# Weaving the adaLN products of a four-layer diffusion backbone: other rates in layers 1 and 2, and layer 0's scale and shift all on TensorE

## The chip, the cores and the metric

The kernel runs on one core of one Trainium2 chip. The metric is device time in microseconds, from the median of three runs. The profile is one further execution of the same program, taken by the hardware profiler. Engines are named as the profile names them: PE is TensorE (PEld its weight loads), DVE VectorE, ACT ScalarE, POOL GpSimd, SP the SyncE queue that issues nearly all DMAs.

## The reference

Two streams of 256 tokens of width 2048, a context (stream 0) and a latent (stream 1), pass through four layers. Their mixers are, in turn, a Fourier transform over tokens and channel groups, a bidirectional mLSTM, grouped-query attention, and the Fourier mixer again. Every layer begins with a modulated norm whose shift, scale and gate come from one conditioning vector per stream:

```python
sc, sc_ctx = silu(c), silu(c_ctx)
for i in range(4):
    shift, scale, gate = split(sc @ ada_w[i] + ada_b[i], 3)        # ada_w[i]: 2048 x 6144
    hx = rmsnorm(x, norm_g[i]) * (1 + scale) + shift
    shift_c, scale_c, gate_c = split(sc_ctx @ ada_w[i] + ada_b[i], 3)
    hc = rmsnorm(ctx, norm_g[i]) * (1 + scale_c) + shift_c
    y_x, y_c = mixer(hx, hc)              # layer 0: (fourier(h) * silu(h @ w_gate)) @ w_out
    x = x + gate * y_x
    ctx = ctx + gate_c * y_c              # not after the last layer
return rmsnorm(x, final_g)
```

The lines `sc @ ada_w[i]` and `sc_ctx @ ada_w[i]` are the adaLN products. `ada_w` is 50 MB of fp32 per layer, read once, for two vectors: it is all memory traffic and hardly any arithmetic. Everything else is matmul of 256 or 512 tokens with 2048-wide weights.

## The kernel before

Activations lie transposed: channel on partitions, token on the free axis, 16 tiles of 128 channels x 512 tokens. All large products run in three passes of fp32r: an operand is split into a rounded part and a remainder (`h`, `l` for activations, `wh`, `wl` for weights), and PE adds h*wh, h*wl and l*wh. ACT makes the rounded part, DVE the remainder.

`gemm` (L262) computes one 512-wide block of outputs over all 16 channel tiles: 8 weight tiles (`wraw`, 512 KB each, two channel tiles in each) and four PSUM banks, 192 matmuls of 512 columns. `make_w` (L244) loads the next weight tile, has ACT round it (L253) and DVE subtract (L254); four raw buffers and three pairs `wh`, `wl` make the prefetch. The weight blocks follow in a fixed list (L238): in layer 0 four blocks of the gate projection and four of the out projection, in layer 1 four pairs of heads with the four blocks qk, v, o, z each and then four out blocks, in layer 2 k, v, four q, four z, four out, in layer 3 four gate and four out.

PE's order is the order in which the program is written. What other engines do, and the order of the DMAs on the SP queue, a planner puts in order, by program order and its own costs; `issue_after(pace[-1])` (L213) holds an adaLN instruction on DVE behind the newest weight split. Woven work is kept in three queues of Python generators, `fill`, `bg` and `adq` (class `Weave`, L91). `run` (L120) steps through a gemm, which yields 32 times, and at each yield gives each queue a credit; a whole credit takes one step of that queue. The credits are the constants of line 27 and 28. `finish` takes all steps up to a key at once, and so sets a deadline.

The adaLN products have two forms:

- `ada_pe` (L170), a chunk of 256 outputs for both vectors: four loads of 512 KB (`araw`, ring of 4), 32 matmuls of 32 weight columns x 256 (L184), a copy by ACT (L188), two transposes (L192), a reduction on DVE (L194). It yields four times.
- `ada_dve` (L198), rows of `ada_w` transposed: a step is one load of 512 KB (same ring), and for each of `nv` streams one multiply with accumulation on DVE (L214) of 128x1024 against `cb`, the conditioning vectors repeated over all partitions.

Head of layer 0, before: `cb` is made by eight `spread` calls (L225: a diagonal by DVE, four transposes, a copy). Tokens `xt` (4 MB) arrive token-major; ACT squares them (L582), `r0` is the inverse norm, DVE scales them (L636). Then a loop over eight pairs `k2` of channel tiles (L637 to L647): scale chunk, shift chunk, then `turned(k2)` is queued on `fill`, which transposes two channel tiles (L612), modulates and splits them, and takes four pieces of the first gemm. Scale and shift are `ada_pe` chunks, but for the shift of `k2` in `DV0` = 2, 4, 6, which is `ada_dve`. At k2 = 1, 3, 5 a Fourier group (`mixed`) is queued on `mixes`. After the loop the first gemm ends, and three more gate blocks and four out blocks follow. During these, at rate BR0, the 4 gate chunks of layer 0 (`ga0`) and the second half of layer 1's scale and shift chunks (`l1`, from `order[NPE1:]`) run on DVE, and at rate AR0 the first half of layer 1's on PE (`adq`, eight `ada_pe` chunks).

Layer 1 onward: all adaLN products are `ada_dve`, queued on `bg` in the order ga1, l2, ga2, l3, ga3, with 32, 64, 32, 64 and 32 steps; ga1 and l2 do two streams in a step, the others one. They are woven at BR1 = 0.3 in every block of layer 1 (L947 to L971), 0.25 in layer 2 (L1112, L1123, L1134), 0.12 in its out projection. Deadlines: ga1 before the out projection of layer 1, l2 after it, ga2 and l3 likewise around layer 2's. In layer 2 the k and q blocks end in `qk_norm` (L1005), a chain of ACT and DVE operations on the PSUM bank, whose result PE transposes (L1036) for the attention steps woven in next.

Of the kernel before, what the change touches and what calls it, by code (L numbers as in the profile page):

```python
# [48 lines left out]
def _build(tc, nc, top, A, out):  # L49
# [119 lines left out]

    def ada_pe(l, s, c, cpad, place):  # L170
# [3 lines left out]
        for k2 in range(2):  # L174
            raws = []
            for kq in (2 * k2, 2 * k2 + 1):
                pp, tag, bufs = next(place[0])
                raw = pp.tile([P, 2, 512], F32, tag=tag, name="araw", bufs=bufs)
                Q.dma_start(raw, A["ada_p"][l, s * 8 + c, kq])
                raws.append(raw.rearrange("p a b -> p (a b)").rearrange("p (q n) -> p q n", q=4))  # L180
            for i, rv in enumerate(raws):
                kq = 2 * k2 + i
                for q in range(4):
                    T.matmul(ps[32 * q:32 * q + 32, :256], cpad[:, 4 * kq + q, :], rv[:, q, :],  # L184
                             start=kq == 0, stop=kq == 3)
            yield 1
# [375 lines left out]
    with ExitStack() as st:  # L562
# [11 lines left out]
        ss = p0.tile([P, 4, 4], F32, name="ss")
        xt = []
        for j in range(4):
            x = p0.tile([P, 4, 512], F32, tag="xf", name="xt", bufs=5)
            Q.dma_start(x, A["xtok"][j])
            xt.append(x)
            for i in range(4):  # L580
                junk = p0.tile([P, 512], F32, tag="mu2", name="junk", bufs=2)
# [786 lines left out]
```

## Time and profile before

| | us |
|---|---|
| time, median of 3 runs (lowest to highest) | 2164.38 (2164.37 to 2164.82) |
| the profiled execution's own time | 2165.99 |
| its span, first to last instruction | 2164.1 |
| PE busy in the span | 2094.9 |
| DVE busy | 1523.5 |
| ACT busy | 813.8 |
| mean granted TensorE clock | 0.986 |

451.5 MB move in the span, nearly all of it read. A busy PE is not always a PE at full speed: matmuls overlap, and in stretches where the clock is granted at half the same matmul takes twice as long. So PE's busy time is read together with the row of the granted clock, and a stage is judged by its own rows, not by the share over the whole span.

### The profile page before, as it was taken

What the parts mean: (1) busy time and instruction counts of PE and PEld (TensorE: products, weight loads), DVE (VectorE), ACT (ScalarE), POOL (GpSimd) and SP (SyncE); (2) the same over time, 40 slices, a digit from 0 to 9 for tenths busy, and PEclk for the clock granted to TensorE, in tenths of its full rate; (3) what the DMA queues carried; (4) which work ended last, traced back from release to release, by engine and by line L of the source; (5) the groups of instructions that cost most, each with busy time, mean ns of one, the idle gap of its engine ahead of it and who ended that gap; (6) DMA issues with size and microseconds to landing.
All of it is one profiled execution on the core that took longest, in us unless ns stands there. A gap on an engine that the chain in (4) does not pass through costs nothing. (4 is left out here: it accounts for less than half of the span.)

```text
span 2164.1 us, 29349 instructions
## 1 busy us (share of the span) xinstructions
PE 2094.9 (97%) x11190; PEld 1728.6 (80%) x11190; DVE 1523.5 (70%) x2793; ACT 813.8 (38%) x1338; POOL 17.3 (1%) x29
## 2 busy tenths in 40 slices
PE   6899999999999999999999999999999999999998
PEld 3568777788788888888888888888777777999986
DVE  4867898856697778787664667646665766777666
ACT  4332242224333323322332343224345554545444
POOL 0000000000000000000000000000000000000000
PEclk7999999999999999999999999999999999999999
DMA  9775778972465666576555667763464556764464
GB/s 341 279 265 194 251 273 286 320 261 94 156 205 175 204 202 196 186 230 214 195 191 199 199 222 247 273 215 98 146 218 148 183 190 205 240 208 137 156 195 147
DMA packets 126126, 451.51 MB, mean 209 GB/s; under 512 B 14224, under 2 KB 16784, under 8 KB 123296
## 3 DMA queue, kind: packets, MB, share of 16 engines
q1 hardware_dynamic: 125696, 448.71, 61.7%
q8 instruction: 88, 1.44, 0.3%
q10 hardware_dynamic: 288, 0.92, 0.1%
q14 instruction: 54, 0.44, 0.1%
HBM read 435.91 MB, written 13.66 MB: 208 GB/s over the span
## 5 line engine op out<-in xcount | busy, mean ns | idle before, releaser
L254 DVE TENSOR_TENSOR wl<-wraw,wh 128x1024 fp32r<-128x1024 f32 x400 | 488.7, 1222 | 438.4 <-ACT wh L253 427.2
L295 PE MATMUL acc<-h,wh 128*128 128x512 f32 (+1 forms) x1936 | 688.5, 356 | 6.1 <-ACT h L392 3.9
L253 ACT CAST wh<-wraw 128x1024 fp32r<-128x1024 f32 x400 | 419.4, 1049 | 720.5 <-PE acc L295 617.9
L295 PE MATMUL acc<-l,wh 128*128 128x512 f32 (+1 forms) x1936 | 670.9, 347 | 3.7 <-DVE l L358 1.9
L295 PE MATMUL acc<-h,wl 128*128 128x512 f32 (+1 forms) x1936 | 669.7, 346 | 1.0 <-DVE wl L254 0.9
L295 PE MATMUL acc<-wh,h 128*128 128x512 f32 x1024 | 428.7, 419 | 5.3 <-DVE am L217 3.7
L295 PEld LDWEIGHTS acc<-h,wh 128*128 128x128 f32 x1936 | 367.0, 190 | 61.9 <-issue 11.5
L295 PEld LDWEIGHTS acc<-l,wh 128*128 128x128 f32 x1936 | 366.6, 189 | 51.8 <-DVE l L393 3.5
L295 PEld LDWEIGHTS acc<-h,wl 128*128 128x128 f32 x1936 | 367.1, 190 | 45.1 <-issue 1.7
L295 PE MATMUL acc<-wh,l 128*128 128x512 f32 x1024 | 401.8, 392 | 0.5 <-DVE l L393 0.5
L295 PE MATMUL acc<-wl,h 128*128 128x512 f32 x1024 | 400.6, 391 | 0.0
L214 DVE SCALAR_TENSOR_TENSOR araw<-araw,cb 128x1024 f32<-128x1024 f32 x300 | 365.4, 1222 | 1.9
L295 PEld LDWEIGHTS acc<-wh,h 128*128 128x128 f32 x1024 | 193.5, 189 | 54.7 <-issue 17.1
L295 PEld LDWEIGHTS acc<-wl,h 128*128 128x128 f32 x1024 | 193.6, 189 | 45.3 <-issue 8.4
L295 PEld LDWEIGHTS acc<-wh,l 128*128 128x128 f32 x1024 | 193.0, 188 | 43.1 <-DVE l L393 1.4
L214 DVE SCALAR_TENSOR_TENSOR ajunk<-araw,cb 128x1024 f32<-128x1024 f32 x172 | 209.9, 1220 | 0.0
L184 PE MATMUL xb<-araw,cpad 128*32 128x256 f32 x672 | 56.2, 437 | 15.3 <-DMA araw<-in_ada_p_dram 15.2
L184 PEld LDWEIGHTS xb<-araw,cpad 128*32 128x32 f32 x672 | 17.7, 116 | 44.5 <-DMA araw<-in_ada_p_dram 27.4
L392 ACT ACTIVATE h<-mu,ada 128x256 fp32r<-128x256 f32 x80 | 36.9, 502 | 35.9 <-DVE mu L391 35.9
L845 PE MATMUL xb<-v,wt 128*128 128x256 f32 x192 | 46.7, 379 | 0.0
L450 ACT ACTIVATE sq<-rn 128x256 f32<-128x256 f32 (+1 forms) x48 | 24.7, 515 | 55.4 <-DVE rn L444 53.4
L905 ACT ACTIVATE jk<-yp 128x256 f32<-128x256 f32 x32 | 13.3, 416 | 78.0 <-DVE yp L903 78.0
(223 smaller groups left out, 1485.4 us busy)
## 6 DMA issues: line engine op xcount, KB each, us to landing
araw<-in_ada_t_dram SPq DMA_DIRECT2D x300, 512.0 KB, 5.0
wraw<-in_w1in_dram SPq DMA_DIRECT2D x128, 512.0 KB, 4.0
araw<-in_ada_p_dram SPq DMA_DIRECT2D x84, 512.0 KB, 5.4
wraw<-in_w2in_dram SPq DMA_DIRECT2D x80, 512.0 KB, 3.6
wraw<-in_w0g_dram SPq DMA_DIRECT2D x32, 512.0 KB, 5.6
wraw<-in_w0o_dram SPq DMA_DIRECT2D x32, 512.0 KB, 5.5
wraw<-in_w1o_dram SPq DMA_DIRECT2D x32, 512.0 KB, 4.2
wraw<-in_w2o_dram SPq DMA_DIRECT2D x32, 512.0 KB, 4.0
```

Source lines behind the costliest of these rows:

```text
L184: T.matmul(ps[32 * q:32 * q + 32, :256], cpad[:, 4 * kq + q, :], rv[:, q, :], start=kq == 0, stop=kq == 3)
L214: V.scalar_tensor_tensor(o, rv, 1.0, cb[:, v + 2 - nv, part], ALU.mult, ALU.mult, accum_out=am[:, v, i, hf:hf + 1])
L253: S.copy(wh, raw)
L254: pace.append(V.tensor_tensor(wl, raw, wh.bitcast(F32), ALU.subtract).ins)
L295: T.matmul(o, lhsT, rhs, start=start, stop=stop)
L392: S.activation(h[:, c], u, AF.Identity, bias=ada[:, l, SH, s, kt:kt + 1])
L450: S.activation(sq[:, c], rn[:, b, c], AF.Square)
L845: T.matmul(po[:, :256], wt[:, 128 * k:128 * k + 128], c.v[:, k, 256 * hh:256 * hh + 256], start=k == 0, stop=k == nb - 1)
L905: S.activation(jk, ys, AF.Square, accum_out=c.ssq[:, 4 * hh + i:4 * hh + i + 1])
```

## The change

- Layer 0's head: all sixteen scale and shift chunks are `ada_pe` (`DV0` is gone). In k2 < 4 their loads land not in the ring `araw` but in the buffers `l8` to `l15`, which the head does not need yet; each 512 KB come as two loads of 256 KB (`land_l`).
- Layer 0's gate products (`ga0`, and behind them `l1`) are queued ahead of the loop, and DVE takes steps of them at rate BRS = 0.5 in k2 = 1 to 4.
- `cb` is no longer spread by PE: 16 KB of `crow` are loaded repeated to all partitions (2 MB into SBUF), and ACT applies SiLU.
- Tokens: squares and scaling are shared between ACT and DVE; all 64 transposes come at k2 = 0 (`turn`), and the results are parked in the buffers `h0` to `h15`, from which `modulated` reads. The pieces of the first gemm come one k2 earlier; the first weight tile is loaded at k2 = 0.
- Layer 1's products on PE go from eight chunks to four (NPE1 4 to 2); two more groups (16 steps) of them go to DVE. AR0 goes from 0.17 to 0.09.
- Rates: layer 1 by pair and block instead of 0.3 throughout, its out projection 0.5, layer 2 none in v and q and 0.25 in z as before.

```diff
-DV0 = (2, 4, 6)
-NPE1, CORE1, ATT = 4, 0.4, 1.2
-MIX3, MIX0, MIX1, FR0, BR0, BR1, AR0 = 0.55, 0.9, 0.7, 0.8, 0.34, 0.3, 0.17
+NPE1, CORE1, ATT = 2, 0.4, 1.2
+MIX3, MIX0, MIX1, FR0, BR0, AR0, BRS = 0.55, 0.55, 0.7, 0.55, 0.34, 0.09, 0.5
+BR1 = ((0, 0.35, 0.25, 0.25), (0.35, 0.35, 0.25, 0.25), (0.4, 0.4, 0.3, 0.3), (0.5, 0.5, 0.35, 0.35))
+BR1O, BR2 = 0.5, 0.25
...
+    def land(pp, tag, bufs):
+        def get(src):
+            raw = pp.tile([P, 2, 512], F32, tag=tag, name="araw", bufs=bufs)
+            Q.dma_start(raw, src)
+            return [raw[:, 0, :], raw[:, 1, :]]
+        return get
+
+    def land_l(kt):
+        def get(src):
+            raws = [hlp.tile([P, 512], F32, tag=f"l{k}", name=f"lraw{k}") for k in (kt, kt + 1)]
+            for i in range(2):
+                Q.dma_start(raws[i], src[:, i, :])
+            return raws
+        return get
...
-        for v in range(2):
-            for j in range(4):
-                o = cb[:, v, 512 * j:512 * j + 512]
-                drain(spread(lambda ps, o=o: V.tensor_copy(o, ps), cvec[:, v, 4 * j:4 * j + 4]))
...
+            if j == 3:
+                S.activation(dummy, one1, AF.Sqrt)
             for i in range(4):
-                S.activation(junk, x[:, i, :], AF.Square, accum_out=ss[:, i, j:j + 1])
+                if i % 2:
+                    S.activation(junk, x[:, i, :], AF.Square, accum_out=ss[:, i, j:j + 1])
+                else:
+                    V.scalar_tensor_tensor(junk, x[:, i, :], 1.0, x[:, i, :], ALU.mult, ALU.mult,
+                                           accum_out=ss[:, i, j:j + 1])
...
-            def turned(k2):
-                for kt in (2 * k2, 2 * k2 + 1):
...
-                        T.transpose(ps[:, 128 * t:128 * t + 128], xt[j][:, t, 128 * i:128 * i + 128], ident)
...
-                if 0 < k2 <= 6:
-                    for _ in range(4):
-                        next(first)
-                        yield
+            def turn(j):
+                for t in range(4):
+                    if t % 2:
+                        S.activation(xt[j][:, t, :], xt[j][:, t, :], AF.Copy, scale=r0[:, t:t + 1])
+                    else:
+                        V.tensor_scalar(xt[j][:, t, :], xt[j][:, t, :], r0[:, t:t + 1], None, ALU.mult)
+                for i in range(4):
+                    ps = bank()
+                    for t in range(4):
+                        T.transpose(ps[:, 128 * t:128 * t + 128], xt[j][:, t, 128 * i:128 * i + 128], ident)
+                    x = hlp.tile([P, 512], F32, tag=f"h{4 * j + i}", name=f"xT{4 * j + i}")
+                    (S.copy if i % 2 else V.tensor_copy)(x, ps)
+                    xT.append(x)
+            def modulated(k2):
...
+                def pieces():
+                    if k2 < 6:
+                        for _ in range(4):
+                            next(first)
+                            yield
+                return pieces()
...
+            spare = cycle(land_l(kt) for kt in (8, 10, 12, 14))
+            bg.add("ga0", ada_chain([(0, GA, j, 2) for j in range(4)]))
+            bg.add("l1", ada_chain([(1, s, j, 2) for s, j in order[NPE1:]]))
             for k2 in range(8):
                 for s in (SC, SH):
-                    for _ in ada_dve(0, s, 2 * k2, 2, 2) if s == SH and k2 in DV0 else ada_pe(0, s, k2, cpad, [slots]):
-                        fill.give(FR0)
-                        mixes.give(MIX0)
+                    for n, _ in enumerate(ada_pe(0, s, k2, cpad, [spare if k2 < 4 else slots])):
+                        if k2 == 0:
+                            if n == 1:
+                                for j in range(4):
+                                    if (j > 0) == (s == SH):
+                                        turn(j)
+                            if s == SH and n == 1:
+                                make_w()
+                                Q.dma_start(cb, A["crow"].to_broadcast([P, 2 * D]).rearrange("p (v k) -> p v k", v=2))
+                                for v in range(2):
+                                    S.activation(cb[:, v, :], cb[:, v, :], AF.Silu)
+                                Q.dma_start(cst[:, C_CD:], A["cst"][:, C_CD:])
+                        else:
+                            if k2 < 5:
+                                bg.give(BRS)
+                            fill.give(FR0)
+                            mixes.give(MIX0)
                 fill.finish(f"t{k2 - 1}")
-                fill.add(f"t{k2}", turned(k2))
+                fill.add(f"t{k2}", modulated(k2))
...
-            run(gemm(hl, "A", 0, 512, c.done[0]) if p else first, 0.5, BR1 if p else 0)
+            run(gemm(hl, "A", 0, 512, c.done[0]) if p else first, 0.5, BR1[p][0])
...
-            "p (a b) -> p a b", a=4), resid[1], 0, [(0.5, BR1)] * 4, norm=norm)
+            "p (a b) -> p a b", a=4), resid[1], 0, [(0.5, BR1O)] * 4, norm=norm)
...
-        run(gemm(hl, "B", 0, 512, done_vv), 1.0, 0.25)
+        run(gemm(hl, "B", 0, 512, done_vv), 1.0, 0)
...
-            run(gemm(hl, "B", 256, 512, done_q), ATT, 0.25)
+            run(gemm(hl, "B", 256, 512, done_q), ATT, 0)
...
-            run(gemm(hl, "B", 256, 512, done_z2), ATT, 0.25)
+            run(gemm(hl, "B", 256, 512, done_z2), ATT, BR2)
```

More of the change, by code (lines that the diff above doesn't have):

```diff
@@ L2 @@
 from contextlib import ExitStack, nullcontext
-from itertools import repeat
+from itertools import cycle, repeat
 import concourse.bass as bass
@@ L174, in ada_pe @@
         for k2 in range(2):
[L175 to L180, printed above, removed]
+            raws = [next(place[0])(A["ada_p"][l, s * 8 + c, kq]) for kq in (2 * k2, 2 * k2 + 1)]
             for i, rv in enumerate(raws):
@@ L183, in ada_pe @@
                 for q in range(4):
-                    T.matmul(ps[32 * q:32 * q + 32, :256], cpad[:, 4 * kq + q, :], rv[:, q, :],
-                             start=kq == 0, stop=kq == 3)
+                    T.matmul(ps[32 * q:32 * q + 32, :256], cpad[:, 4 * kq + q, :],
+                             rv[q // 2][:, 256 * (q % 2):256 * (q % 2) + 256], start=kq == 0, stop=kq == 3)
             yield 1
@@ L632, in _build @@
             mixes = Weave()
[L633 to L636 removed]
+            slots = repeat(land(ap_, "araw", ARAW))
+            spare = cycle(land_l(kt) for kt in (8, 10, 12, 14))
+            order = [(s, j) for s in (SC, SH) for j in range(4)]
+            bg.add("ga0", ada_chain([(0, GA, j, 2) for j in range(4)]))
+            bg.add("l1", ada_chain([(1, s, j, 2) for s, j in order[NPE1:]]))
             for k2 in range(8):
                 for s in (SC, SH):
[L639 to L641 removed]
+                    for n, _ in enumerate(ada_pe(0, s, k2, cpad, [spare if k2 < 4 else slots])):
[15 more added lines that the diff above has]
+                            mixes.give(MIX0)
                 fill.finish(f"t{k2 - 1}")
[L643 to L645 removed]
+                fill.add(f"t{k2}", modulated(k2))
                 if k2 in (1, 3, 5):
@@ L652, in _build @@
             run(first, MIX1)
-            order = [(s, j) for s in (SC, SH) for j in range(4)]
             place = [slots]
-            bg.add("ga0", ada_chain([(0, GA, j, 2) for j in range(4)]))
-            bg.add("l1", ada_chain([(1, s, j, 2) for s, j in order[NPE1:]]))
             for s, j in order[:NPE1]:
@@ L663, in _build @@
         pa = pool(st, "l0a", reuse_waits="tile")
-        place[0] = repeat((pa, "praw", 2))
+        place[0] = repeat(land(pa, "praw", 2))
         for g in range(2, 4):
@@ L959, in _build @@
             fill.add(f"core{p}", core(c))
-            run(gemm(hl, "B", 0, 512, c.done[2]), CORE1, BR1)
-            run(gemm(hl, "A", 0, 512, c.done[3], used=load_y if p == 3 else None), CORE1, BR1)
+            run(gemm(hl, "B", 0, 512, c.done[2]), CORE1, BR1[p][2])
+            run(gemm(hl, "A", 0, 512, c.done[3], used=load_y if p == 3 else None), CORE1, BR1[p][3])
             fill.finish(f"core{p}")
@@ L1316, in _layout @@
     r["xT"] = np.ascontiguousarray(x.T.reshape(KT, 128, NT).transpose(1, 0, 2))
+    r["crow"] = np.concatenate([g["c_ctx"], g["c"][0]])[None]
     r["cvec"] = np.ascontiguousarray(
```

21 lines of the change are left out of this document (8 added, 13 removed).

## The prediction

> **What bounds the kernel now.** I read the summary first, then the busy time by stage, then who waits for whom in the stages where PE isn't full. The page's first part:
>
> ```profile
> span 2164.1 us, 29349 instructions
> PE 2094.9 (97%) x11190; PEld 1728.6 (80%) x11190; DVE 1523.5 (70%) x2793; ACT 813.8 (38%) x1338; POOL 17.3 (1%) x29
> ```
>
> PE sets the end: 69 us of the span are without it. So there are two ways to gain, less work on PE or less of those 69 us, and each stage must be looked at for itself. The view of busy time by stage (columns: stretch, length, busy time of each engine with its instructions, granted clock, DMA share, GB/s):
>
> ```profile
> 0.00:20.00 20.00, 9.96 (x56) 6.75 (x56) 11.98 (x28) 13.42 (x37) 0.20 (x4) 0.91 0.90 351
> 20.00:45.00 25.00, 17.04 (x132) 5.26 (x128) 11.37 (x32) 4.55 (x10) 0.00 (x0) 0.64 0.93 328
> 45.00:153.50 108.50, 92.21 (x660) 64.75 (x656) 76.03 (x195) 38.82 (x85) 0.00 (x0) 0.91 0.79 280
> 174.00:222.30 48.30, 48.30 (x222) 39.66 (x221) 38.48 (x73) 12.34 (x19) 0.00 (x0) 1.00 0.66 226
> 222.30:459.50 237.20, 237.05 (x1198) 185.93 (x1197) 202.04 (x343) 64.64 (x83) 0.00 (x0) 1.00 0.82 292
> 560.80:915.80 355.00, 355.00 (x1612) 284.93 (x1611) 283.08 (x542) 121.77 (x210) 11.07 (x15) 1.00 0.60 193
> 915.80:1004.70 88.90, 88.90 (x402) 73.63 (x401) 68.00 (x110) 26.93 (x37) 0.00 (x0) 1.00 0.67 217
> 1305.60:1438.00 132.40, 132.40 (x593) 109.66 (x592) 84.84 (x145) 36.11 (x44) 0.00 (x0) 1.00 0.73 251
> 1534.30:1717.40 183.10, 172.04 (x790) 136.55 (x789) 113.18 (x163) 82.64 (x118) 0.00 (x0) 0.96 0.55 181
> ```
>
> The first three rows are layer 0's head up to the last shift chunk: PE lacks 34.3 of 153.5 us, its clock is granted at 0.64 for a time, and DMA is 0.79 to 0.93 busy. The next rows are the rest of layer 0 and layer 1: PE is full, DVE at 85% (202.04 of 237.20) or less. The last is layer 2's v and q blocks: 11.1 us without PE at clock 0.96. The waits in the head, PE's and then the SP queue's (us, times, longest):
>
> ```profile
> PE xb L184 <- DMA araw<-in_ada_p_dram: 15.2, 18, 3.5
> PE xb L233 <- DVE adiag L228: 8.1, 3, 5.1
> ```
>
> ```profile
> SPq L179 <- PE xb L184: 36.5, 28, 4.9
> SPq L179 <- DVE araw L214: 29.9, 9, 7.7
> ```
>
> PE waits for adaLN loads, and the queue that issues them waits for buffers held by PE or by DVE. The head is a matter of bytes and of how many loads are in flight.
>
> **The change part by part.**
>
> *Layer 0's body, PE: gain 9.2 us.* Four `ada_pe` chunks leave a stretch in which PE is full. The groups of instructions there, and one entry of PE's timeline:
>
> ```profile
> L184 PE MATMUL xb<-araw,cpad 128*32 128x256 f32 x224 | 15.0, 385 | 0.0
> L192 PE MATMUL xb<-cst,ar 128*128 128x128 f32 x12 | 2.3, 270 | 0.0
> ```
>
> ```profile
> 230.50 1.07 PE L184 MATMUL xb<-araw,cpad 128*32 128x256 f32 x16
> ```
>
> Sixteen of a chunk's 32 matmuls take 1.07 us (15.0 / 224 x 16 is the same), and a pair of transposes at most 0.38 (2.3 / 6), less where it overlaps its neighbours: 2.3 us a chunk, 9.2 for four. Their share of DVE and ACT (a reduction, a copy) is below a microsecond each. DVE gets 16 steps of `l1` in exchange, but 16 of `ga0`'s 32 steps have gone to the head (32 credits of 0.5), so the body's 64 steps stay 64. DVE's 202 us then stand against 228: 89%, still room. If DVE can't keep that, the gain shrinks; I keep 4 to 9.5.
>
> *Layer 0's head: loss 4 us, the least certain term.* Bytes moved by 153.5 us: 351 x 20 + 328 x 25 + 280 x 108.5 = 45.6 MB. The three `DV0` chunks are the same bytes in either form. New are `crow` (2.1 MB) and sixteen `ga0` loads (8.4 MB), less about 1 MB that ran ahead for them already: 55.1 MB. Against that stand more loads in flight: four in `l8` to `l15` beside four of `araw` in k2 = 1 to 4. The rates that the trace has:
>
> ```profile
> GB/s 415 350 293 390 307 162 163 258 162 329 372 279 314 387 285 168 391 397 396 207 27 254 337 334 20 317 252 400 228 305 372 397 192 62 248 340 273 290 343 205
> araw<-in_ada_p_dram SPq DMA_DIRECT2D x32, 512.0 KB, 4.9
> ```
>
> ```profile
> l<-ytd SPq DMA_DIRECT2D x12, 256.0 KB, 3.7
> araw<-in_ada_t_dram SPq DMA_DIRECT2D x8, 512.0 KB, 5.0
> ```
>
> (45 to 153.5 us in 40 slices, with the head's chunk loads; then two load sizes from the end of layer 1; the last column is us to landing.) At the head's own mean, 297 GB/s, the bytes take 186 us; at 328, the rate when PE did nothing but wait for loads, 168; at 351 157; at 397, of single slices, 139. With eight in flight for two thirds of the bytes I take 345: 160 us, 6 later than now. The first gemm's pieces come one k2 earlier, so fewer are left behind the last chunk: by the order of yields now three pieces of six matmuls, 4 us at 0.23 apart (timeline below). PE already waits for the last splits there, and without pieces before it longer:
>
> ```profile
> PE acc L295 <- DVE l L358: 1.2, 2, 0.8
> ```
>
> I let that give back half of the 4 us. Head: +6 - 2 = +4. The bounds are 139 us (-17) and 186 us (+30).
>
> The other parts of the head cost nothing, since PE has 34 us to spare there: three more chunks (6.9 us), against 32 transposes of `spread` that go; the 64 token transposes only move forward, into the time in which the second and third chunk land. What DVE is given (24 products of 1.2 us in the loop become 32, half the squares and 8 copies) meets a DVE that is busy 76 of 108.5 us. PE's own work up to there, 119.2 us by the three rows and about as much after, stays below the loads' time in every case.
>
> The Trainium skill, page "DMA: Bandwidth & Descriptors", section "Rules for kernel authors", says to coalesce small transfers and to move at least 1 MiB in a DMA; its section "Bandwidth" gives 341 GB/s at 1 MB and 138 at 64 KB. An estimate between these by halvings is 290 for 512 KB and 240 for 256 KB, by which the 16.8 MB that the change loads in halves would take 12 us more, and the sum would be 12 us worse. The rows above speak for less: a half lands in 3.7 us, a whole in 5.0, and both halves are in flight at once.
>
> *Layer 1's rates: 0.* At 32 yields a block, steps to the end of the out projection go from 173 (0.3 x 32 x 18) to 213 (32 x 5.15, the sum of the new rates, and 0.5 x 32 x 3). The tightest place is pair 2's qk and v, where 0.4 for 0.3 gives 6.4 steps more of two products over both blocks. What DVE does there for the products, and in the out projection:
>
> ```profile
> 915.80:1004.70 88.90, 45.48 (x76) 1.00 0.67 217
> 1305.60:1438.00 132.40, 33.74 (x56) 1.00 0.73 251
> ```
>
> (The stage view for L214 alone; half of the instructions are the reading of an accumulator.) A product is 1.20 us. Pair 2: 68.0 + 12.8 x 1.20 = 83.4 of 88.9 us. Out projection: 96 x 0.2 = 19.2 steps of one product, 84.8 + 23 = 108 of 132.4. Neither is full, and PE waits for nothing in these stretches now. If the last few per cent stall the weight split, a few us are lost: 0 to +5.
>
> *Layer 2's v and q without products: gain 8 us.* PE's waits from 1534.3 to 1717.4, then DVE and PE as the v block begins:
>
> ```profile
> PE xb L1063 <- ACT pe L1057: 4.0, 2, 3.3
> PE acc L295 <- DVE am L217: 3.7, 1, 3.7
> PE xb L1036 <- DVE rb L1028: 3.1, 2, 2.0
> ```
>
> ```profile
> 1535.46 1.20 DVE L214 SCALAR_TENSOR_TENSOR araw<-araw,cb 128x1024 f32<-128x1024 f32 x1
> ...
> 1540.20 1.19 DVE L214 SCALAR_TENSOR_TENSOR araw<-araw,cb 128x1024 f32<-128x1024 f32 x1
> ...
> 1541.92 0.68 DVE L1016 TENSOR_TENSOR xn<-acc,r 128x512 f32<-128x512 f32 x1
> ```
>
> ```profile
> 1538.41 0.39 PE L295 MATMUL acc<-wl,h 128*128 128x512 f32 x1
> 1538.64 0.40 PE L295 MATMUL acc<-wh,l 128*128 128x512 f32 x1
> 1542.75 0.76 PE L295 MATMUL acc<-wh,h 128*128 128x512 f32 x1 [3.71 <-DVE am L217]
> 1543.31 0.63 PE L295 MATMUL acc<-wl,h 128*128 128x512 f32 x1
> ```
>
> The 3.7 us wait is for the last bank of k (L1016), queued on DVE behind products. Two of them lie in its way, 2.4 us. The 3.1 us for L1028 are the same chain for the first q block, also with products between; without them I count all 3.1. The 4.0 us for L1057 are exps behind other work of ACT, and stay. After the long wait the next matmul comes 0.56 us later instead of 0.23: the clock is at half. Clock 0.96 over 183.1 us is 7.3 us lost. Of the 11.1 us of waits 5.5 go, so half of it, 3.7; I count 2.5, since a slow spell can begin at a wait that stays. 2.4 + 3.1 + 2.5 = 8. Bounds: 2 (only what stands directly in front) and 18 (all waits and the clock).
>
> A part of this stretch where only the two L1036 waits stand, the longer 2.0 us:
>
> ```profile
> 1607.30:1644.00 36.70, 33.65 (x156) 25.59 (x154) 25.25 (x37) 19.71 (x30) 0.00 (x0) 0.95 0.56 189
> ```
>
> The clock fell there too. The Trainium skill, page "TensorE: Matmul & The Clock Gate", Part 1, puts the halving after an idle window of about 3.4 us; by it the 7.3 us would hang on the waits of 3.7 and 3.3 us alone, about half on the one that goes, and the sum would be 1 us better. The row's 0.95 doesn't agree with a window that long.
>
> *Sum.* -9.2 + 4 + 0 - 8 = -13 us. On the profiled execution's 2165.99 us (span 2164.1 and 1.9 around it) that is 2153; the median of the runs is 1.6 lower, so 2151.
>
> **The rivals.**
>
> 1. *The head's loads decide* (slower). DMA stays at the head's mean rate, because SP is one queue: a `ga0` load that waits for a buffer held by DVE (29.9 us of such waits now) stops every scale and shift load behind it, and in k2 = 4 both share one ring again. The head costs up to +30 instead of +4: 2151 + 26 = 2177. It decides against the change from a rate of 319 GB/s down: then the last chunk comes at 173 us, and the 17.2 us of the other terms are used up. For it: 280 GB/s in the loop now. Against it: 328 with four loads in flight and an idle PE.
> 2. *Layer 2's waits stay*, because weight splits and ACT's rounding stand in the chain too: only 2 of 8 us come, 2157.
> 3. *DVE fills up in layer 0 and layer 1*, the planner putting the products elsewhere than the rates say, so that the four chunks taken from PE come back as waits for weight splits: no gain in the body and up to 5 us lost in layer 1, 2151 + 9 + 5 = 2165, no change. Against it: 89% and 94%.
> 4. *The loads run at 397 GB/s*: the head gains 17, 2130. The slices that reach this are few.
>
> **How the numbers follow.** Forecast 0.50, rival 1 0.18 (half of it at a small loss or none), rival 2 0.17, rival 3 0.08, rival 4 0.07. About 0.2% (4.3 us) is what a measurement of this kernel can tell from no change. Faster: 0.50 + 0.17 + 0.07, and little of the others: 0.76. Same: rival 3 and the near part of rival 1, 0.11. Slower: 0.13. The range reaches to rival 4 and to the middle of rival 1: 2131 to 2171. The likeliest case by itself holds 2141 to 2160.
>
> **What would show it.** Right: the last L184 of the head at about 160 us with 55 MB moved before it; 128 matmuls of L184 after the head instead of 256, and gemms there 2.3 us shorter for each chunk gone; in layer 1 no wait of PE for L254; in v and q no L214 on DVE and no wait for the last k bank above 1.5 us. Wrong: a last chunk after 173 us, SP waiting for L214 longer than 30 us in it, or PE waiting for weight splits anywhere from 560 to 1438 us. The forecast falls with the head's rate first, and then with layer 2.

## The result and the profile after

The changed kernel takes 2169.34 us (median of 8 runs) against 2164.6 us of the kernel before (8 runs as well): ratio 1.0024, 95% interval 1.0014 to 1.0035, so it is slower by 3 to 8 us. The forecast was 2151. The profiled execution took 2168.66 us. In the changed file the lines of the planned work stand some 13 further down: the chunk matmul is L197 (was L184), the chunk's loads L184 (halves, into the `l` buffers) and L175 (the ring), the product on DVE L227 (L214) with its load L220, the weight tile's load, rounding and subtraction L263, L266 and L267 (L250, L253, L254), the gemm matmul L308 (L295), the split of `u` into `h` and `l` L370 and L371 (L357, L358).

The first part of the page after:

```profile
span 2166.9 us, 29317 instructions
PE 2090.5 (96%) x11124; PEld 1726.6 (80%) x11124; DVE 1534.1 (71%) x2803; ACT 822.5 (38%) x1341; POOL 19.0 (1%) x29
```

PE has 4.4 us less work and 7.2 us more without work. The view of busy time by stage after (stretch, length, busy time of PE, PEld, DVE, ACT and POOL, granted clock, DMA share, GB/s); then the same head stretches of the kernel before:

```profile
20.00:60.00 40.00, 32.92 (x233) 17.16 (x233) 26.10 (x54) 22.85 (x36) 0.00 (x0) 0.96 1.04 397
60.00:120.00 60.00, 47.49 (x318) 32.38 (x318) 43.02 (x99) 16.83 (x36) 0.00 (x0) 0.81 0.80 286
120.00:174.20 54.20, 46.03 (x347) 30.47 (x346) 28.98 (x85) 18.05 (x39) 0.00 (x0) 0.89 0.83 301
...
244.60:476.80 232.20, 229.12 (x1096) 183.31 (x1095) 200.29 (x336) 63.63 (x80) 0.00 (x0) 1.00 0.77 267
575.50:930.40 354.90, 354.90 (x1611) 284.94 (x1610) 279.71 (x535) 121.67 (x210) 10.37 (x15) 1.00 0.58 190
930.40:1019.30 88.90, 88.90 (x401) 73.65 (x400) 82.34 (x136) 27.10 (x37) 0.00 (x0) 1.00 0.76 253
1320.30:1452.80 132.50, 132.50 (x594) 109.62 (x593) 105.40 (x186) 35.84 (x44) 0.00 (x0) 1.00 0.88 325
1549.00:1719.40 170.40, 165.80 (x792) 132.85 (x790) 87.58 (x111) 82.49 (x119) 0.00 (x0) 1.00 0.38 124
```

```profile
20.00:60.00 40.00, 28.27 (x197) 12.87 (x194) 19.04 (x48) 9.70 (x21) 0.00 (x0) 0.67 0.90 325
60.00:120.00 60.00, 52.05 (x374) 36.43 (x374) 43.42 (x115) 21.38 (x48) 0.00 (x0) 0.94 0.77 274
120.00:153.60 33.60, 29.02 (x222) 20.80 (x220) 24.93 (x66) 12.29 (x27) 0.00 (x0) 0.95 0.80 275
```

The stages begin where PE starts a gemm, so their shift is the ledger of the change:

| stretch | before, us | after, us | difference | forecast |
|---|---|---|---|---|
| start to the second gemm (layer 0's head and first gemm) | 174.0 | 196.3 | +22.3 | +4 |
| from there to layer 1 (layer 0's body) | 335.7 | 328.1 | -7.6 | -9.2 |
| layer 1 | 975.8 | 975.8 | 0.0 | 0 |
| layer 2's k block | 48.8 | 48.8 | 0.0 | none |
| layer 2's v and q | 183.1 | 170.4 | -12.7 | -8 |
| the rest | 446.7 | 447.5 | +0.8 | none |

The head spoils the sum. Its last scale or shift chunk ends at 174.2 us instead of 153.6. DMA starts at 397 GB/s between 20 and 60 us and then falls to 286, and PE's clock falls with it, to 0.81. PE's and SP's waits in the head after (PE from 0 to 200 us, SP from 0 to 174; us, times, longest):

```profile
PE xb L197 <- ACT junk L595: 16.0, 1, 16.0
PE xb L197 <- DMA araw<-in_ada_p_dram: 9.2, 7, 2.9
PE acc L308 <- ACT h L370: 6.4, 3, 3.0
PE acc L308 <- ACT wh L266: 6.3, 2, 3.3
PE xb L197 <- DMA lraw<-in_ada_p_dram: 3.1, 1, 3.1
PE acc L308 <- DVE wl L267: 2.5, 2, 1.9
PE acc L308 <- DVE l L371: 1.9, 3, 1.5
```

```profile
SPq L175 <- PE xb L197: 31.5, 16, 5.6
SPq L184 <- PE xb L197: 20.2, 16, 7.1
SPq L175 <- DVE araw L227: 13.5, 3, 7.5
```

Before, PE's waits were for loads and for `spread`; now 17.1 us of them stand at L308, at the pieces of the first gemm, which wait for their own operands: `h` and `l` just modulated, `wh` and `wl` just loaded (before, these four came to 4.4 us). SP's waits for L227, by which the slower rival was to be told, fell from 29.9 to 13.5 us.

Layer 0's body and layer 2, after: the chunk matmuls between 196.3 and 524.4 us in the view of groups, PE's only wait from 380 to 477 us, and PE's waits in v and q.

```profile
L197 PE MATMUL xb<-araw,cpad 128*32 128x256 f32 x128 | 8.6, 385 | 0.0
```

```profile
PE acc L308 <- DVE wl L267: 3.1, 2, 1.7
```

```profile
PE acc L308 <- DVE xn L1059: 2.2, 1, 2.2
PE xb L1079 <- DVE rb L1071: 1.4, 2, 1.0
PE xb L1106 <- ACT pe L1100: 1.0, 1, 1.0
```

### The profile page after: what moved, and what is told of

The parts are those of the page before. It is cut to its first block, busy times and chain, and to the rows that moved or that the text cites. A ratio compares the mean times of both kernels' runs of the same rounds, so it can differ in the third digit from the quotient of the medians.

```text
span 2166.9 us, 29317 instructions
## 1 busy us (share of the span) xinstructions
PE 2090.5 (96%) x11124; PEld 1726.6 (80%) x11124; DVE 1534.1 (71%) x2803; ACT 822.5 (38%) x1341; POOL 19.0 (1%) x29
## 5 line engine op out<-in xcount | busy, mean ns | idle before, releaser
L267 DVE TENSOR_TENSOR wl<-wraw,wh 128x1024 fp32r<-128x1024 f32 x400 | 489.7, 1225 | 405.4 <-ACT wh L266 402.4
L308 PE MATMUL acc<-h,wh 128*128 128x512 f32 (+1 forms) x1936 | 691.6, 357 | 16.5 <-ACT h L370 6.4
L266 ACT CAST wh<-wraw 128x1024 fp32r<-128x1024 f32 x400 | 419.3, 1049 | 713.2 <-PE acc L308 560.5
L308 PE MATMUL acc<-l,wh 128*128 128x512 f32 (+1 forms) x1936 | 675.1, 349 | 3.7 <-DVE l L371 1.9
L308 PE MATMUL acc<-h,wl 128*128 128x512 f32 (+1 forms) x1936 | 673.1, 348 | 5.6 <-DVE wl L267 5.6
L308 PE MATMUL acc<-wh,h 128*128 128x512 f32 x1024 | 426.5, 417 | 3.5 <-DVE xn L1059 2.2
L308 PEld LDWEIGHTS acc<-h,wh 128*128 128x128 f32 x1936 | 369.4, 191 | 73.4 <-issue 9.9
L308 PEld LDWEIGHTS acc<-l,wh 128*128 128x128 f32 x1936 | 369.0, 191 | 53.6 <-DVE l L371 4.5
L308 PEld LDWEIGHTS acc<-h,wl 128*128 128x128 f32 x1936 | 369.8, 191 | 51.3 <-DVE wl L267 7.4
L308 PE MATMUL acc<-wh,l 128*128 128x512 f32 x1024 | 400.6, 391 | 0.5 <-DVE l L406 0.5
L308 PE MATMUL acc<-wl,h 128*128 128x512 f32 x1024 | 399.1, 390 | 0.0
L227 DVE SCALAR_TENSOR_TENSOR araw<-araw,cb 128x1024 f32<-128x1024 f32 x304 | 369.7, 1223 | 10.2 <-DMA araw<-in_ada_t_dram 7.7
L308 PEld LDWEIGHTS acc<-wh,h 128*128 128x128 f32 x1024 | 192.5, 188 | 52.1 <-issue 14.6
L308 PEld LDWEIGHTS acc<-wl,h 128*128 128x128 f32 x1024 | 192.7, 188 | 44.4 <-issue 8.4
L308 PEld LDWEIGHTS acc<-wh,l 128*128 128x128 f32 x1024 | 192.2, 188 | 42.7 <-DVE l L406 1.3
L227 DVE SCALAR_TENSOR_TENSOR ajunk<-araw,cb 128x1024 f32<-128x1024 f32 x176 | 215.0, 1222 | 7.0 <-DMA araw<-in_ada_t_dram 7.0
L197 PE MATMUL xb<-lraw,cpad 128*32 128x256 f32 x256 | 29.9, 437 | 19.8 <-ACT junk L595 16.0
L888 PEld LDWEIGHTS xb<-v,wt 128*128 128x128 f32 x192 | 36.3, 189 | 6.1
```

Source lines behind the costliest of these rows:

```text
L227: V.scalar_tensor_tensor(o, rv, 1.0, cb[:, v + 2 - nv, part], ALU.mult, ALU.mult, accum_out=am[:, v, i, hf:hf + 1])
L266: S.copy(wh, raw)
L267: pace.append(V.tensor_tensor(wl, raw, wh.bitcast(F32), ALU.subtract).ins)
L308: T.matmul(o, lhsT, rhs, start=start, stop=stop)
L888: T.matmul(po[:, :256], wt[:, 128 * k:128 * k + 128], c.v[:, k, 256 * hh:256 * hh + 256], start=k == 0, stop=k == nb - 1)
```

## The experiments

Theory A: what the head moves is what it costs, `ga0`'s 16 loads (8.4 MB) above all. Theory B: the head lost its slack. (Later expectations name theories of their own.) A piece of the first gemm that isn't ready stops PE, which works in program order; the chunk behind it can't free its buffers; SP, one queue, stands before the next load; the rate falls. All runs, with the head read from each run's profile (e1 to e4, e5 to e8 and e9 to e12 ran beside the kernel before with 2165.92, 2166.02 and 2166.37 us; the expectations count after's last chunk from 173.8 us, where its last matmul starts, the table has its end):

| run | time, us | ratio to before, 95% interval | last chunk ends | mean GB/s until then | second gemm starts |
|---|---|---|---|---|---|
| before | | | 153.6 | 298 | 174.0 |
| after | 2169.34 | 1.0024 (1.0014 to 1.0035) | 174.2 | 323 | 196.3 |
| e1 rates only | 2154.39 | 0.9943 (0.9928 to 0.9958) | 152.1 | 301 | 172.5 |
| e2 no ga0 in head | 2155.1 | 0.9950 (0.9935 to 0.9965) | 155.4 | 312 | 177.3 |
| e3 pieces late | 2160.21 | 0.9971 (0.9959 to 0.9984) | 165.4 | 334 | 187.7 |
| e4 weights ahead | 2160.89 | 0.9977 (0.9965 to 0.9989) | 168.1 | 335 | 190.3 |
| e5 late and ahead | 2154.81 | 0.9948 (0.9932 to 0.9965) | 159.2 | 348 | 181.6 |
| e6 no ga0, late, ahead | 2147.88 | 0.9925 (0.9904 to 0.9946) | 141.1 | 335 | 163.5 |
| e7 ga0's loads only | 2159.33 | one run | 166.6 | 334 | 188.5 |
| e8 ga0's products only | 2154.1 | one run | 159.6 | 303 | 181.8 |
| e9 eight in flight | 2144.08 | 0.9894 (0.9879 to 0.9909) | 140.0 | 341 | 163.9 |
| e10 all in halves | 2147.3 | 0.9907 (0.9890 to 0.9923) | 145.3 | 325 | 169.2 |
| e11 products to gates | 2151.36 | one run | 159.3 | 345 | 181.6 |
| e12 one group more | 2144.58 | 0.9896 (0.9881 to 0.9911) | 143.6 | 329 | 165.9 |

### Rates only (e1)

The kernel before with the new rates of layers 1 and 2 and nothing of layer 0.

```diff
+BR1 = ((0, 0.35, 0.25, 0.25), (0.35, 0.35, 0.25, 0.25), (0.4, 0.4, 0.3, 0.3), (0.5, 0.5, 0.35, 0.35))
+BR1O, BR2 = 0.5, 0.25
...
-        run(gemm(hl, "B", 0, 512, done_vv), 1.0, 0.25)
+        run(gemm(hl, "B", 0, 512, done_vv), 1.0, 0)
...
```

> The kernel before, with the change's rates for layers 1 and 2 and nothing else of it. By the two traces the stretch from layer 2's v block to its out projection is 13.5 us shorter after the change, layer 1 the same, layer 3's first block 1.5 us longer. If these belong to the rates, this kernel is 12 us faster than before (2152 to 2153 us), with its head unchanged (first gate block ends at 174). If part of it came from what the head does to the order of the products, it gains less, 5 to 8 us.

Measured: 0.57% faster, by the interval 9.1 to 15.6 of 2166 us. Layer 1 keeps its length (976.4 us; 975.8 before); the second q block takes 33.4 us (before 36.7), the third 31.4 (37.5), as they do after, the v block 49.4 (before 51.3, after 47.9). The gain of layer 2 belongs to the rates alone, and the loss to layer 0's head.

The 1.5 us between the two v blocks are the clock's. PE waits 2.2 us for the last k bank in both; here the matmuls behind that wait come 0.42 to 0.46 us apart instead of 0.23 (PE's timeline, then the stage view):

```profile
1539.87 0.66 PE L298 MATMUL acc<-wh,h 128*128 128x512 f32 x1 [2.17 <-DVE xn L1019]
```

```profile
1540.00:1543.50 3.50, 3.50 (x9) 2.74 (x10) 1.83 (x3) 0.80 (x1) 0.00 (x0) 0.51 0.05 16
```

All 13 profiles with the new rates have this wait of 2.2 us. Right behind it the clock is halved in four of them (e1, e2, e5, e11: v block 49.4 to 49.5 us) and not in the other nine (47.8 to 47.9).

### ga0 out of the head (e2)

```diff
-NPE1, CORE1, ATT = 2, 0.4, 1.2
+NPE1, CORE1, ATT = 4, 0.4, 1.2
-MIX3, MIX0, MIX1, FR0, BR0, AR0, BRS = 0.55, 0.55, 0.7, 0.55, 0.34, 0.09, 0.5
+MIX3, MIX0, MIX1, FR0, BR0, AR0, BRS = 0.55, 0.55, 0.7, 0.55, 0.34, 0.17, 0.0
```

> The kernel after, with no step of ga0 in the head (BRS 0) and the body's products as before (NPE1 4, AR0 0.17). Theory A (ga0's loads and products displace the scale and shift chunks): the head's last chunk comes 18 us sooner, at about 156 us instead of 173.8, the body costs its 7.6 us again, in all 2159 us. Theory B (PE waits for tiles modulated just before and for weight tiles, since the pieces of the first gemm follow one k2 earlier): the head stays within 4 us of 173.8, in all 2173 to 2177 us.

Measured: the last chunk comes 18.8 us earlier than after, and the body is back at 335.8 us (the profile is of the slowest of four runs, 2158.95 us). But it moves 48.4 MB at 312 GB/s, more slowly than after's 323, with PE's clock at 0.91 to 0.94, and PE's waits at L308 are still 10.8 us (7.5 of them for `h`). So theory A has a part, and bytes aren't all of it.

### Pieces later, weights ahead, both (e3, e4, e5)

e3 puts the pieces back by one k2, as before the change. e4 loads a weight tile at each k2 ahead of its pieces, with `ga0` where the change has it; since `make_w` now stands ahead of the modulation, the tile's rounding on ACT and its subtraction on DVE move ahead too. e5 is both.

```diff
                 def pieces():
-                    if k2 < 6:
+                    if 0 < k2 <= 6:
                         for _ in range(4):
... (e4, further up in the file)
             def modulated(k2):
+                if k2 < 6:
+                    make_w()
```

> The kernel after, with the pieces of the first gemm one k2 later, as they were before (0 < k2 <= 6). Theory A: the head stays, 2169 us, plus or minus 2. Theory B: PE's waits for h (6.4 us) and l (1.9 us) in the head go, the last chunk comes 8 us sooner, about 2161 us; up to 4 us may come back behind the last chunk, where the later pieces then stand.

> The kernel after, with each weight tile of the first gemm loaded one k2 ahead. Theory A: no change, 2169 us. Theory B: PE's waits for wh (6.3 us) and wl (2.5 us) in the head go, the last chunk comes 8 to 9 us sooner, 2160 us. The bytes of the head are the same in either case, so a gain here speaks against a head bound by bytes alone.

> The kernel after, with both: pieces of the first gemm one k2 later and weight tiles one k2 ahead; ga0 stays in the head. The first gate block ended at 196.3 us in the profile of after, at 187.7 with late pieces alone, at 190.3 with early weight tiles alone. If these waits are all that stands between the head and its 56 MB at 397 GB/s, both together give 181 and 2154 us. If the bytes of ga0 hold it at some 330 GB/s (about 168 us for the last chunk), the two don't add up: 186 to 188, 2160 us.

Measured: the last chunk ends 8.8 us earlier with e3, 6.1 with e4, 15.0 with both: in these profiles the two mends add up. (For e4 8 to 9 were expected: the waits for `wh` and `wl` went, those for `h` and `l` grew from 8.3 to 10.9 us.) e5 by stretch, and PE's waits from 0 to 200 us:

```profile
20.00:60.00 40.00, 29.74 (x216) 13.83 (x211) 26.27 (x52) 24.05 (x38) 0.00 (x0) 0.83 1.04 398
60.00:120.00 60.00, 51.02 (x371) 33.43 (x370) 49.36 (x119) 19.45 (x43) 0.00 (x0) 0.94 0.92 334
120.00:159.20 39.20, 36.89 (x305) 24.88 (x303) 20.06 (x65) 13.51 (x32) 0.00 (x0) 1.00 0.91 318
```

```profile
PE xb L197 <- DMA araw<-in_ada_p_dram: 10.8, 9, 2.3
PE xb L197 <- DMA lraw<-in_ada_p_dram: 9.0, 3, 4.3
PE acc L308 <- DVE l L371: 1.3, 2, 0.9
```

From 60 to 120 us DMA moves 334 GB/s instead of 286, with the same loads. The waits at L308 are down from 17.1 us to 2.2 (1.3, and 0.9 for `h`); what PE waits for now is loads, 19.8 us. This head runs at 348 GB/s and ends its chunks at 159.2 us with 55.3 MB moved: the prediction had 345, 160 and 55.1. (The expectation's 181 us for the second gemm came true at this rate, not at its 397.) How the slack was lost can be read in the kernel after itself, at one place: the timelines of PE, ACT and DVE, SP's queue, and the view by stage (start, us, engine, line, idle before):

```profile
75.82 0.83 PE L197 MATMUL xb<-lraw,cpad 128*32 128x256 f32 x12
79.94 0.50 PE L308 MATMUL acc<-h,wh 128*128 128x512 f32 x1 [3.29 <-ACT wh L266]
82.32 0.79 PE L308 MATMUL acc<-h,wl 128*128 128x512 f32 x1 [1.88 <-DVE wl L267]
...
84.75 1.94 PE L197 MATMUL xb<-lraw,cpad 128*32 128x256 f32 x16
```

```profile
58.62 1.04 ACT L266 CAST wh<-wraw 128x1024 fp32r<-128x1024 f32 x1 [1.49 <-DMA wraw<-in_w0g_dram]
...
76.35 1.58 ACT L645 ACTIVATE u<-xT,ada 128x256 f32<-128x256 f32 x3 [2.27 <-DVE ada L167]
...
78.86 1.03 ACT L266 CAST wh<-wraw 128x1024 fp32r<-128x1024 f32 x1
```

```profile
81.05 1.22 DVE L267 TENSOR_TENSOR wl<-wraw,wh 128x1024 fp32r<-128x1024 f32 x1
```

```profile
70.88 0.42 SPq L263 DMA_DIRECT2D wraw<-in_w0g_dram  x1
71.66 2.55 SPq L184 DMA_DIRECT2D lraw<-in_ada_p_dram  x4
74.30 0.92 SPq L220 DMA_DIRECT2D araw<-in_ada_t_dram  x2
76.24 11.37 SPq L184 DMA_DIRECT2D lraw<-in_ada_p_dram  x8
```

```profile
76.00:80.00 4.00, 0.71 (x13) 0.19 (x5) 4.00 (x10) 3.65 (x7) 0.00 (x0) 1.00 1.02 375
80.00:84.00 4.00, 2.12 (x5) 1.52 (x6) 3.97 (x6) 0.41 (x1) 0.00 (x0) 0.55 0.97 381
84.00:88.00 4.00, 4.00 (x23) 1.85 (x23) 3.05 (x6) 0.37 (x1) 0.00 (x0) 0.60 0.28 89
```

The weight tile was issued at 70.88 us and landed 6.1 us later, at 77.0; PE needs it at 76.6. So only some 0.3 us of the wait of 3.29 are the load's. From 76.35 to 78.9 us ACT modulates two channel tiles (L645, L370), whose `h` the same pieces need (the first at 78.4), and only then rounds the weights; on DVE a Fourier operation and the split of `u` (L660, L371) stand ahead of the subtraction, and PE waits another 1.88 us. An earlier wait, 3.01 us from 56.7 on, is the load's: ACT itself waited for it (58.62). With e4 the waits for `wh` and `wl` go, with e3 most of those for `h`. Meanwhile the loads already issued go on arriving (375 GB/s). The chunk follows at 84.75, at half speed (1.94 us for sixteen matmuls that take 1.07). All that time SP has eight loads to issue into buffers which that chunk holds: its run lasts from 76.24 to 87.61 us, and between 84 and 88 us DMA moves 89 GB/s. A wait of 5 us on PE has become a hole in the loads. In e3, e4 and e5 SP's waits for L197 at these loads fall from 20.2 us to 9.3, 9.9 and 6.0.

### Both (e6)

e2, e3 and e4 together: no `ga0` in the head, pieces late, weights ahead.

> The same two mends, with no ga0 in the head and the body's products as before the change (as in the run without ga0: first gate block ended at 177.3). By theory B the remaining waits for h, l, wh and wl (10.8 us in that run) go: the block ends at 167 to 170, 7 us less than before the change, and the whole takes 2146 us. If the head then is bound by its 48 MB and by PE's own order, it ends at 174 to 177 and the whole takes 2153.

Measured: 2147.88 us, faster than both kernels, with the lowest median so far (its interval overlaps those of e1, e2 and e5). By stretch:

```profile
20.00:60.00 40.00, 32.38 (x246) 17.25 (x246) 17.77 (x38) 24.71 (x39) 0.00 (x0) 0.96 1.01 378
60.00:120.00 60.00, 58.03 (x476) 39.98 (x472) 30.79 (x96) 24.56 (x56) 0.00 (x0) 1.00 0.87 312
120.00:141.10 21.10, 19.42 (x171) 12.57 (x169) 11.19 (x32) 7.20 (x16) 0.00 (x0) 1.00 0.87 312
```

PE is busy 109.8 of 121.1 us; the loads hardly decide any more. Against e5 the second gemm starts 18.1 us earlier and the body is 7.6 us longer (335.7 against 328.1): with the slack restored, moving 16 steps of `ga0` into the head and four chunks off PE loses 10.5 us in the two profiles, 7 in the medians. That splits the head's +22.3 us: the new head without either burden starts the second gemm 10.5 us earlier than before (163.5 against 174.0), `ga0` puts 18.1 on it, and the lost slack 14.7 (e5 against after). Taken in the other order the two give 19.0 (e2) and 13.8. Both theories hold. That the two simply add up isn't shown: e6's profile is of its fastest run (2143.45 us) and e2's of its slowest, and by the medians e6 gains 7.2 us on e2, not the profiles' 15.5. So each share is known to some 5 us.

PE's time up to the second gemm, from the same four profiles:

| us | after | e2 | e5 | e6 |
|---|---|---|---|---|
| waits at L308, for the pieces' operands | 17.1 | 10.8 | 2.2 | 2.2 |
| waits for chunk loads | 12.3 | 9.1 | 19.8 | 9.2 |
| other time without work | 17.6 | 17.0 | 18.1 | 18.2 |
| busy, with 1012 or 1013 matmuls | 149.3 | 140.4 | 141.5 | 133.9 |

`ga0` costs PE waits for loads where the slack is there (e5 against e6, 10.6 us), and 7.6 us of slower matmuls. The lost slack costs the waits at L308 themselves and 6.5 to 7.9 us of slower matmuls. PE doesn't wait longer for loads when the slack is lost: beside `ga0` half of the waits at L308 fall into time in which it would have waited for loads anyway.

### ga0's loads alone, its products alone (e7, e8)

e7 keeps the 16 loads of `ga0` in the head and leaves their products out; e8 keeps the products, on `cb` in place of the loads.

```diff
+        if (l, s) == (0, GA) and k0 < 8:
+            V.memset(am, 0.0)
...
-                for v in range(nv):
+                for v in range(nv if (l, s) != (0, GA) or k0 >= 8 else 0):
```

```diff
+                free = (l, s) == (0, GA) and k0 < 8
...
-                Q.dma_start(rv, A["ada_t"][l, s * KT + k0 + i][:, part])
+                rv = cb[:, 1, part] if free else raw.rearrange("p a b -> p (a b)")
+                if not free:
+                    Q.dma_start(rv, A["ada_t"][l, s * KT + k0 + i][:, part])
```

> The kernel after, with ga0's loads of the head kept and the 32 products on them left out (half of layer 0's gate is left out of the result). With them gone DVE has 37 us less to do in the head. If the bytes displace the chunk loads, the head's last chunk stays within 4 us of 173.8. If DVE's products delay what PE waits for, and hold the buffers for which the queue waits, it comes 12 to 18 us sooner.

> The kernel after, with ga0's 32 products of the head kept, on data that is there already, and their sixteen loads left out (half of layer 0's gate is computed from other data). If the bytes decide, the last chunk comes 12 to 18 us sooner than 173.8, as in the run without ga0 (155.4). If DVE's products decide, it stays within 4 us.

Measured: without the products the last chunk ends 7.6 us earlier than after, without the loads 14.6, without both (e2) 18.8. Both matter and they overlap; the loads weigh twice as much. e7 lies between its two expectations. The products held buffers of the ring (SP's 13.5 us) and stood on DVE before the splits, but without them PE's waits at L308 don't shrink: 11.4 us for `wh` alone in e7. Each of the two is one run with one profile, so the split between them is rough.

### Eight buffers (e9)

The ring of four, idle in e6 up to k2 = 3, takes every second load.

```diff
-            spare = cycle(land_l(kt) for kt in (8, 10, 12, 14))
+            spare = cycle(g for kt in (8, 10, 12, 14) for g in (land_l(kt), land(ap_, "araw", ARAW)))
```

> e6 with the head's adaLN loads of k2 < 4 landing by turns in l8 to l15 and in the ring of four, which stands idle there: eight loads of a pair in flight instead of four. Theory A (queue: the rate falls because SP stands behind buffers that PE still holds): SP's 19.5 us of waits for L197 by the l-buffers' loads shrink below 10, the rate in 20 to 60 us rises from 378 GB/s towards 397, the last chunk ends 3 to 8 us before e6's 141.1, and the kernel takes 2140 to 2146 us. Theory B (e6's head is PE's own work, 110 of the 121 us from 20 to 141): the last chunk stays within 2 us of 141, 2146 to 2149 us.

Measured: from 20 to 60 us the rate rises from 378 to 403 GB/s, and SP's waits for L197 by the `l` buffers' loads, 19.5 us in e6, are down to 1.2 (those by the ring's loads went from 33.7 to 38.0). But the last chunk ends at 140.0 us (141.1) and the second gemm starts at 163.9 (163.5). Theory B of the expectation holds for the head: it is PE's own work by now. The median, 2144.08, lies where theory A had it, 3.8 us below e6's, which ran in another group, and the intervals overlap; the two profiles' spans differ by 0.4 us. A gain isn't shown.

### All loads in halves (e10)

```diff
-            Q.dma_start(raw, src)
+            for i in range(2):
+                Q.dma_start(raw[:, i, :], src[:, i, :])
```

> e6 with the ring's loads for the products on PE in two halves of 256 KB as well, in the head from k2 = 4 on (16.8 MB there) and in the body. If a load of 256 KB is as good as half of one of 512 KB, nothing changes: last chunk at 141 to 142 us, 2147 to 2150 us. If small loads cost what the estimate in the prediction gave for the same 16.8 MB, 12 us, the last chunk comes at about 153 and the time is about 2160.

Measured: 2147.3 us against 2147.88. In the profile the last chunk comes 4.2 us later than in e6's, with PE's clock at 0.97 up to the second gemm instead of 0.99; with runs of e6 between 2143.45 and 2152.07 one profile can't say whether that is the halves. The 12 us that the prediction worked out from the Trainium skill's page "DMA: Bandwidth & Descriptors", section "Bandwidth", for as many bytes isn't there. But e6's head is PE's own work, in which a price of the loads can hide, so what the change itself paid for its halves isn't shown; its own head loaded at 397 GB/s with them for 40 us.

### Products moved to the gate gemms (e11)

e5 with the body's products at other rates.

```diff
-            run(gemm(hl, "A", 0, 512, lambda b, ps: done_g(b, ps, 1)), MIX1, BR0)
+            run(gemm(hl, "A", 0, 512, lambda b, ps: done_g(b, ps, 1)), MIX1, 0.45)
...
-                           [(0, BR0, AR0)] * 3 + [(0, 0, AR0)], gate=lambda: bg.finish("ga0"), norm=norm)
+                           [(0, 0.23, AR0)] * 3 + [(0, 0, AR0)], gate=lambda: bg.finish("ga0"), norm=norm)
```

> e5 with the body's products on DVE at rate 0.45 in the three gate gemms and 0.23 in the first three out gemms, instead of 0.34 in all. Theory A (the 3.1 us of PE's waits for L267 come from the order at the end of an out gemm: its epilogue on DVE and five products stand ahead of the next weight split): the waits in the out gemms go, the body is 3 us shorter, 2151 to 2153 us. Theory B (DVE is full over the body, so work moved is work that stalls elsewhere): waits of 3 us or more for L267 appear in the gate gemms instead, 2154 to 2158 us.

Measured: the 3.1 us of waits for L267 are gone and none came elsewhere in the body, which is 324.9 us long, 3.2 less than e5's and 10.8 less than before. In the kernel after, DVE's timeline at the second of these waits reads:

```profile
424.80 0.87 DVE L457 SCALAR_TENSOR_TENSOR rn<-acc,ada,rold 128x256 f32<-128x256 f32 x2
425.59 1.21 DVE L227 SCALAR_TENSOR_TENSOR araw<-araw,cb 128x1024 f32<-128x1024 f32 x1
...
433.55 1.21 DVE L227 SCALAR_TENSOR_TENSOR araw<-araw,cb 128x1024 f32<-128x1024 f32 x1
434.69 1.21 DVE L267 TENSOR_TENSOR wl<-wraw,wh 128x1024 fp32r<-128x1024 f32 x1
```

From 420.1 to 434.7 us there is no weight split. In the last 10 us of them the end of an out gemm (residual and squares, L457 and L464) and five products stand in front of it. DVE isn't full over the stage (200.29 of 232.20 us); it is its order at the end of a gemm.

### The swap without the head's part (e12)

e6 with six of layer 1's chunks on PE instead of eight, the eight further steps on DVE in the body. (Shown against the kernel after; e6 has 4, 0.34 and 0.17 for NPE1, BR0 and AR0.)

```diff
-NPE1, CORE1, ATT = 4, 0.4, 1.2
+NPE1, CORE1, ATT = 3, 0.4, 1.2
-MIX3, MIX0, MIX1, FR0, BR0, AR0, BRS = 0.55, 0.55, 0.7, 0.55, 0.34, 0.17, 0.0
+MIX3, MIX0, MIX1, FR0, BR0, AR0, BRS = 0.55, 0.55, 0.7, 0.55, 0.39, 0.13, 0.0
```

> e6 with six of layer 1's chunks on PE instead of eight, the eight steps more on DVE in the body (BR0 0.39, AR0 0.13), none in the head: the swap of the change without its price in the head. Two chunks are 4.6 us of PE. If DVE has room (202 + 19 of 233 us): body 4 to 4.6 us shorter than e6's, 2143 to 2144 us. If the order at the ends of gemms decides: waits for L267 of 2 to 5 us, 2146 to 2149 us. If DVE is full: waits over 6 us, 2150 us or more.

Measured: the body takes 332.7 us, 3.0 less than e6's, with 1.7 us of waits for L267 (two, the longest 1.3); 2144.58 us. The body's term lies between the first two expectations, and the median between their times. Of the versions run, e9 and e12 are the fastest, 22 us below before; they can't be told apart.

## Why the prediction was right and wrong, point by point

- **Layer 0's head, +4 forecast, +22.3 measured.** This is the step that failed, and in it two sentences. The first: "the first gemm's pieces come one k2 earlier", taken as a gain of 2 us. The tail behind the last chunk became no shorter (22.1 us after, 22.3 in e3, 20.4 before), and putting the pieces back gains 8.6 us up to the second gemm. The second: the other parts "cost nothing, since PE has 34 us to spare there". Spare time on PE doesn't hide a wait that stands in PE's order ahead of the next chunk, because that chunk frees the buffers for the loads. The pieces' operands were waits of that kind, 17.1 us: `h` and `l` modulated just before, and the weight tile, loaded, rounded and split only when its pieces come. The prediction didn't list them, nor the slower matmuls behind them. The last chunk came at 174.2 us instead of 160. The rate of 345 GB/s with eight loads in flight, on which the forecast of 160 us rested, was chosen between rates of the trace; e5, without those waits, has 348 and 159.2, the changed kernel 323.
- **Whether the head was a matter of bytes.** In part. The forecast took `ga0`'s 8.4 MB into the total but never priced the swap by itself: four chunks off PE, worth 9.2 us by the prediction, for 8.4 MB, which at its own 345 GB/s are 24 us of a stage bound by loads. e5 against e6 is that price: 18.1 us in the head for 7.6 in the body by the profiles, 14.5 for 7.6 by the medians.
- **Layer 0's body, -9.2 forecast, -7.6 measured.** Mechanism right, 128 chunk matmuls instead of 256 (the row quoted above). The size was off both ways: without waits the four chunks are worth 10.8 us (e11), and 3.2 came back as waits for L267. "DVE's 202 us then stand against 228: 89%, still room" was true of the stage and not of a gemm's end.
- **Layer 1's rates, 0.** Right: 975.8 us in both, PE full in each quoted stretch, DVE 82.34 of 88.90 and 105.40 of 132.50 us where 83.4 and 108 were worked out. PE waits for no weight split there.
- **Layer 2's v and q, -8 forecast, -12.7 measured.** Mechanism right, e1 shows that it is the rates; two terms mis-sized. The waits fell from 11.1 to 4.6 us, 6.5 against 5.5: the wait for the last bank (L1059 now) still has 2.2 us where 1.3 were left over, and the one at the q blocks (L1071) 1.4 where none was; but the waits for exps on ACT, which were to stay, fell from 4.0 to 1.0. And the clock came back whole, 0.96 to 1.00: PE's busy time fell from 172.04 to 165.80, 6.2 us, where 2.5 were counted. 1.5 us of that is luck: in four of the 13 profiles with the new rates the clock fell once more, behind the same wait of 2.2 us (e1). So the idle window of about 3.4 us on the Trainium skill's page "TensorE: Matmul & The Clock Gate", Part 1, doesn't hold here as a bound, as the prediction's row of 0.95 with waits of 2.0 us had shown already: behind a wait of 2.2 us the clock can fall, and need not.
- **Rival 1** had the place, the sign and its last chunk after 173 us (174.2), though at 323 GB/s and not at 319 or below, since 56.3 MB had moved instead of 55.1. Its mechanism wasn't the one. It blamed loads that wait for buffers held by DVE; those waits fell to 13.5 us, and e5, which still has 14.0 of them, loads at 348 GB/s. **Rival 2** is out (layer 2 gained more than forecast). **Rival 3** came true at two gemm ends, for 3 us. **Rival 4's** 397 GB/s was reached from 20 to 60 us, and not kept.
- **The sum.** -7.6 and -12.7 in place of -17.2 is 3 us better than forecast; the head, 18 us worse, took all of it.

What stays open: how `ga0`'s 18 to 19 us split into its loads and its products (e7 and e8 overlap, and are one run each), and which part of the change makes the head without `ga0` 10.5 us shorter than before; no run took apart its loads, its transposes, `crow`, and the lower rates of its woven work (FR0 0.8 to 0.55, MIX0 0.9 to 0.55), which stand in the diff alone. How much of the slower matmuls is the clock's is open too: no run changed it by itself.

## What to carry to other kernels

In a stage whose loads are issued by one queue into buffers that PE frees, price every piece of work put between two chunks by whether its operands are there, not by PE's spare time: a wait of 3 to 5 us there stops the queue, and the matmuls behind it ran slower as well. Work moved from a stage bound by PE to one bound by loads costs its bytes at that stage's rate, which is to be set against its gain before anything else. And a share of 85 or 90% of an engine over a stage says nothing about the end of a gemm, where the epilogue and the woven work meet: look at the timeline there.

## What the runs showed of the hardware

The price of the waits in the head came about twice, once as waits and once as slower matmuls. The kernel after and e6 run the same matmuls up to the second gemm (1012 and 1013), and PE is without work for 47.0 and 29.6 us there; yet its busy time differs by as much again:

```profile
0.00:196.30 196.30, 149.33 (x1012) 96.73 (x1013) 117.73 (x299) 78.51 (x156) 0.20 (x4) 0.90 0.82 300
```

```profile
0.00:163.50 163.50, 133.90 (x1013) 87.67 (x1014) 80.62 (x231) 77.81 (x156) 0.20 (x4) 0.99 0.85 309
```

Of the 32.8 us between the two, 17.4 are waits and 15.4 are the same matmuls, slower, at a mean clock of 0.90 instead of 0.99. After the wait of 3.29 us above the clock was 0.55 for 4 us and 0.60 for the next 4. The mean clock alone doesn't measure this: e9's head has 131.1 us of busy PE at 0.96, less than e6's. And a wait needn't be long: right behind the 2.2 us in the v block the clock was halved in four profiles of 13. The second surprise is that loads of 256 KB, enough of them in flight, ran as fast as any here: 397 and 398 GB/s over 40 us in the kernel after and e5, at a DMA share of 1.04, with 34 or 35 halves among 10 or 11 larger loads, and 403 in e9 with halves and wholes by turns, where the mean of the head before was 298.
